# Rotating an 8192 x 8192 array by 90 degrees: 31 chunks of 1024 columns in place of 63 of 512, and a last macro tile that stays whole

## The chip, the cores and the metric

One core of one Trainium2 chip. The metric is device time in microseconds (us), median over runs. The program runs on this one core.

## The reference

```python
# x: 8192 x 8192 float32, k = 1
def reference(x, k):
    return np.rot90(x, k)      # out[i, j] = x[j, 8191 - i]
```

There is no arithmetic: 268.44 MB are read and 268.44 MB written, and on the way each 128 x 128 block is turned.

## The kernel before

The array is cut into 16 macro tiles of 1024 rows by 4096 columns. A macro tile has 8 **row tiles** (128 rows x 4096 columns, one load of 2 MiB each) and gives 8 **output groups** (512 columns of the input, one store of 2 MiB each), numbered 0 to 7.

- The SP queue loads row tiles into two load buffers (`a_pool`; some of the first eight loads go into output buffers that are still free).
- VectorE copies a loaded row tile, column order within blocks reversed, into **chunks** (`r_pool`). A load buffer is free again when all chunks of its row tile are copied.
- TensorE transposes blocks from chunks into PSUM. A chunk is free when all its columns have been transposed.
- ScalarE evicts PSUM into one of three output buffers (`o_pool`) and issues the store.

```python
W = 4096
CH = 512
a_pool = ctx.enter_context(tc.tile_pool(name="a_pool", bufs=2))
r_pool = ctx.enter_context(tc.tile_pool(name="r_pool", bufs=63))
o_pool = ctx.enter_context(tc.tile_pool(name="o_pool", bufs=3))
# ...
# load, for each row tile t of a macro tile:
nc.sync.dma_start(out=a[:], in_=x[r0 + t * P : r0 + (t + 1) * P, c0 : c0 + W])
for j in range(W // CH):
    ar = r_pool.tile([P, CH // P, P], dt, tag="ar")
    nc.vector.tensor_copy(out=ar[:], in_=a[:, j * CH : (j + 1) * CH]...[:, :, ::-1])
    chunks[t, j] = ar
# ...
# store, for each output group i (two halves h of two 128-column blocks):
if i == 0 and (rt == RT or r0 + rows < N):
    for t in range(rt):              # group 0: row tile by row tile, as they come in
        transposes(t, range(G))
# ... groups 1 to 7: block by block over all row tiles
nc.scalar.copy(o[:, G - PW - h : G - h, :], ps[h // PW])
nc.scalar.dma_start(out=dst, in_=o[:, G - done : G - done + S, :])
```

A macro tile of 8 row tiles needs 64 chunks of 512 columns and the pool has 63. And group 0 transposes row tile by row tile while they are loaded, so with chunks of 512 columns (one group wide) the chunks of group 0 are given back during the load, from the first row tile on. The last macro tile is split into two of 4 row tiles (`LAST = [4, 4]`), so that storing its first half overlaps loading its second.

## Time and profile before

| | before |
|---|---|
| median time | 1267.35 us (6 runs, 1266.35 to 1267.61) |
| transfers, 200 to 1200 us | 429 GB/s |
| VectorE copies | 1024 of 512 columns, 421 ns each, busy 355.4 us (28%) |
| ScalarE waiting for TensorE | 29.0 us, 10 times |
| ScalarE waiting for stores to land | 727.0 us, 118 times |

Transfers run at one flat rate and every engine waits for them. The lines are shown in the prediction. A row of the waits reads: who waited, for whom, total us, times, longest; a ScalarE wait for a store to land means that all three output buffers are filled or under way, which is the healthy state here: stores are always pending.

### The profile page before, as it was taken

The numbers are of one execution on the slowest core, as the hardware profiler recorded it, in microseconds if no ns is written. First come the engines' busy times: TensorE is split into PE (matmuls) and PEld (weight loads), VectorE is DVE, ScalarE is ACT, GpSimd is POOL, SyncE is SP. The second block draws the span as 40 slices with busy tenths as digits, with TensorE's granted clock in tenths as the row PEclk, the third lists the DMA queues.
The fourth block names the chain that finished last, engine by engine and source line by source line (L and its number), as shares of the span: only waits on it lengthen the run. The fifth ranks groups of instructions, "written<-read, shape, count | busy, mean of one in ns | idle before, by whom it ended". The sixth has DMA issues, their size and how long they took to land.

```text
span 1266.1 us, 10392 instructions
## 1 busy us (share of the span) xinstructions
PE 718.2 (57%) x4096; PEld 678.6 (54%) x4096; DVE 355.4 (28%) x1024; ACT 466.7 (37%) x257; POOL 0.7 (0%) x6
## 2 busy tenths in 40 slices
PE   1554565556656665556555665555655656556673
PEld 1543455555555555456554655555655655556562
DVE  4423223222232223222232223322232222322210
ACT  0432433433333333343334333343333433343363
POOL 0000000000000000000000000000000000000000
PEclk9977877777776777867778678677686686776797
DMA  9999999999999999999999999999999999999997
GB/s 399 426 428 430 428 429 427 430 429 429 429 429 429 430 428 427 430 429 430 428 430 428 429 429 428 430 428 428 430 430 428 429 429 428 428 428 428 427 399 328
DMA packets 37345, 537.55 MB, mean 425 GB/s; under 512 B 4144, under 2 KB 4144, under 8 KB 4144
## 3 DMA queue, kind: packets, MB, share of 16 engines
q10 hardware_dynamic: 18864, 268.44, 50.0%
q1 hardware_dynamic: 18432, 268.44, 49.7%
q8 instruction: 32, 0.52, 0.2%
q14 instruction: 17, 0.14, 0.0%
HBM read 268.44 MB, written 268.44 MB: 424 GB/s over the span
## 4 chain that ended last, share of the span: by engine, by line
DMA 82%; ACT 14%; PE 1%; issue 1%; ACTq 1%; DVE 0%; SPq 0%
DMA out_dram<-ot 79%; ACT ot L169 14%; DMA a<-in_x_dram 3%; PE pt L148 1%; ACTq L177 0%; DVE ar L108 0%; ACTq L169 0%; SPq L102 0%
## 5 line engine op out<-in xcount | busy, mean ns | idle before, releaser
L148 PE MATMUL pt<-ident,ar 128*128 128x128 f32 x4096 | 718.2, 356 | 528.0 <-ACT ot L169 487.6
L148 PEld LDWEIGHTS pt<-ident,ar 128*128 128x128 f32 x4096 | 678.6, 191 | 567.4 <-ACT ot L169 521.4
L169 ACT COPY ot<-pt 128x2048 f32<-128x2048 f32 x256 | 465.4, 1869 | 756.7 <-DMA out_dram<-ot 727.0
L108 DVE COPY ar<-a 128x512 f32<-128x512 f32 x1024 | 355.4, 421 | 861.1 <-DMA a<-in_x_dram 524.0
L169 ACT ACT_TABLE_LOAD x1 | 1.3, 1283 | 25.5 <-DVE ar L108 25.5
masks.py:199 POOL TENSOR_SCALAR_AFFINE_SELECT ident<-ident 128x128 f32<-128x128 f32 x1 | 0.3, 292 | 0.1
masks.py:197 POOL MEMSET ident<- 128x128 f32 x1 | 0.2, 204 | 0.3 <-POOLq L217 0.3
L217 POOL MEMSET const-bfloat16-1.0<- 128x1 bf16 x1 | 0.1, 102 | 0.0
L217 POOL MEMSET const-uint8-127<- 128x1 uint8 x1 | 0.1, 102 | 0.0
L217 POOL MEMSET const-float32-0.0<- 128x1 f32 x1 | 0.1, 99 | 0.2 <-issue 0.2
L217 POOL MEMSET const-float32-1.0<- 128x1 f32 x1 | 0.1, 99 | 0.0
## 6 DMA issues: line engine op xcount, KB each, us to landing
a<-in_x_dram SPq DMA_DIRECT2D x128, 2048.0 KB, 16.8
out_dram<-ot ACTq DMA_DIRECT2D x125, 2048.0 KB, 25.5
out_dram<-ot ACTq DMA_DIRECT2D x6, 1024.0 KB, 27.3
```

Of the source, the lines that this page charges most:

```text
L108: nc.vector.tensor_copy(out=ar[:], in_=a[:, j * CH : (j + 1) * CH].rearrange("r (b m) -> r b m", m=P)[:, :, ::-1],)
L148: nc.tensor.transpose(ps[w // PW][:, PW - 1 - w % PW, t * P : (t + 1) * P], chunks[t, g * P // CH][:, g % (CH // P), :], ident,)
L169: nc.scalar.copy(o[:, G - PW - h : G - h, :], ps[h // PW])
L217: nc = _bacc.Bacc("TRN2", target_bir_lowering=False, num_devices=1)
```

## The change

What it seems to be for: half as many VectorE copies and a simpler end. With 1024 columns a chunk serves two output groups, a macro tile needs 32 chunks, and the pool has 31.

```diff
-LAST = [4, 4]
-CH = 512
+CH = 1024
 ...
-    tiles = [(r0, RT, c0) for r0 in range(0, N, R) for c0 in range(0, M, W)]
-    r0, _, c0 = tiles.pop()
-    for n in LAST: ...
+    return [(r0, RT, c0) for r0 in range(0, N, R) for c0 in range(0, M, W)]
 ...
-    r_pool = ctx.enter_context(tc.tile_pool(name="r_pool", bufs=63))
+    r_pool = ctx.enter_context(tc.tile_pool(name="r_pool", bufs=31))
 ...
-            S = PW if lead or (end and r0 + rows == N and g0 + G == W // P) else G
+            S = PW if lead or (end and (i == 0 or g0 + G == W // P)) else G
 ...
+    for m in tiles:
+        store(*m, load(*m), m == tiles[-1])
```

(The generators that interleaved the two half tiles are gone; cuts are marked.)

More of the change, by code (lines that the diff above doesn't have):

```diff
@@ L47, in macro_tiles @@
 def macro_tiles(N, M):
-    tiles = [(r0, RT, c0) for r0 in range(0, N, R) for c0 in range(0, M, W)]
-    r0, _, c0 = tiles.pop()
-    for n in LAST:
-        tiles.append((r0, n, c0))
-        r0 += n * P
-    return tiles
+    return [(r0, RT, c0) for r0 in range(0, N, R) for c0 in range(0, M, W)]
 @with_exitstack
@@ L104, in load @@
             )
-            yield chunks
             for j in range(W // CH):
@@ L114, in load @@
                 chunks[t, j] = ar
-            yield chunks
+        return chunks
     def store(r0, rt, c0, chunks, end):
@@ L179, in store @@
                     )
-            yield
     tiles = macro_tiles(N, M)
-    *most, before_last, last = tiles
-    for m in most:
-        *_, chunks = load(*m)
-        for _ in store(*m, chunks, False):
-            pass
-    *_, chunks = load(*before_last)
-    outputs = store(*before_last, chunks, True)
-    rows = load(*last)
-    for _ in range(2 * last[1] - 1):
-        next(rows)
-    next(outputs)
-    chunks = next(rows)
-    for _ in outputs:
-        pass
-    for _ in store(*last, chunks, True):
-        pass
+    for m in tiles:
+        store(*m, load(*m), m == tiles[-1])
 _INS = ['x', 'k']
```

## The prediction

> **What bounds the kernel now.** I read the page first (busy shares and the row of GB/s), then the waits, then one stretch of the timeline in mid-run, then a table of windows over the start and the end. The page:
>
> ```profile
> span 1266.1 us, 10392 instructions
> PE 718.2 (57%) x4096; PEld 678.6 (54%) x4096; DVE 355.4 (28%) x1024; ACT 466.7 (37%) x257; POOL 0.7 (0%) x6
> ...
> GB/s 399 426 428 430 428 429 427 430 429 429 429 429 429 430 428 427 430 429 430 428 430 428 429 429 428 430 428 428 430 430 428 429 429 428 428 428 428 427 399 328
> DMA packets 37345, 537.55 MB, mean 425 GB/s; under 512 B 4144, under 2 KB 4144, under 8 KB 4144
> ```
>
> No engine is busy for more than 57%, and the transfers run flat at 427 to 430 GB/s in 36 of 40 slices. Only the first two slices (the second by a hair) and the last two are lower. So the kernel is a copy through the chip at the rate of the transfers, with an edge at each end. The waits (who waited for whom, total us, times, longest) say the same:
>
> ```profile
> ACT ot L169 <- DMA out_dram<-ot: 727.0, 118, 11.0
> DVE ar L108 <- DMA a<-in_x_dram: 524.0, 82, 10.2
> ...
> DVE ar L108 <- PE pt L148: 337.1, 49, 7.7
> ```
>
> ScalarE waits for stores to land (an output buffer), VectorE waits for loads, and 49 times for TensorE, which is the wait for a free chunk. One cycle of the timeline in mid-run (start, duration, then the instructions and the idle time before):
>
> ```profile
> 587.95 5.28 PE L148 MATMUL pt<-ident,ar 128*128 128x128 f32 x32 [3.02 <-ACT ot L169]
> 589.69 0.55 ACTq L177 DMA_DIRECT2D out_dram<-ot  x1
> 593.21 2.78 DVE L108 COPY ar<-a 128x512 f32<-128x512 f32 x8 [7.08 <-PE pt L148]
> 595.79 3.63 ACT L169 COPY ot<-pt 128x2048 f32<-128x2048 f32 x2 [6.13 <-DMA out_dram<-ot]
> ```
>
> Each 9.8 us one output group (32 transposes, two evictions, a 2 MiB store) leaves, its end frees the 8 chunks of its columns, and VectorE copies one row tile's worth (8 chunks) into them, which frees a load buffer. The next cycles start at 603 and 613 us: one store and one load per 9.8 us, 4.19 MB in 9.8 us = 428 GB/s. The windows (width; busy us of the engines; granted clock, share and GB/s last):
>
> ```profile
> 200.00:1100.00 900.00, 527.74 (x2914) 501.79 (x2912) 254.88 (x736) 332.63 (x184) 0.00 (x0) 0.74 1.01 429
> ...
> 1205.00:1210.00 5.00, 1.28 (x9) 0.89 (x9) 1.61 (x5) 3.63 (x2) 0.00 (x0) 0.90 0.94 398
> 1210.00:1215.00 5.00, 3.98 (x24) 3.75 (x24) 1.29 (x4) 1.42 (x1) 0.00 (x0) 0.76 0.94 400
> 1215.00:1220.00 5.00, 3.92 (x34) 3.64 (x35) 1.49 (x5) 4.33 (x4) 0.00 (x0) 1.00 0.80 338
> ...
> 1258.00:1260.00 2.00, 0.00 (x0) 0.00 (x0) 0.00 (x0) 0.00 (x0) 0.00 (x0) 0.50 0.39 160
> 1260.00:1262.00 2.00, 0.00 (x0) 0.00 (x0) 0.00 (x0) 0.00 (x0) 0.00 (x0) 0.50 0.15 61
> ```
>
> The budget, as time lost against 429 GB/s: 537.55 MB / 429 = 1253.0 us of pure transfer. Start, 0 to 6 us at 106, 287 and 393 GB/s: 2.3 lost. The three windows from 1205 to 1220, as the last load lands: (31 + 29 + 91) x 5 / 429 = 1.8. From 1220 to 1258, stores alone at 413 to 419: 1.1. From 1258 to the end, a few of the 16 transfer engines finishing (160, 61, 41 and 8 GB/s): 8.1 - 1.3 = 6.8. Sum 12.0, so 1265.0 of the 1266.1.
>
> **What the Trainium skill says.** "DMA: Bandwidth & Descriptors", section "Where 436 GB/s comes from", puts the ceiling of the 16 ports at 435.2 GB/s; the trace's 429 is 98.6% of it, so nothing in this change can make the middle faster by as much as 2%. The same page, "Queues, rings and completion order", says that each transfer engine takes turns, packet by packet, between the queues that have work; the trace agrees as far as loads and stores each move 2.1 MB per 9.8 us. It follows that an empty load queue hands its share to the stores and costs nothing while stores are pending. "VectorE: DVE Perf Modes", section "Mode 2×_2P", says that an fp32 copy within SBUF uses both ports for two elements a cycle; here 512 columns take 421 ns, less than the 533 ns of one element per cycle at its 0.96 GHz, so the copy is in that mode.
>
> **The change, part by part.**
> 1. *Half as many copies, twice as wide.* Eight narrow copies take 2.77 us, 346 ns each. Two per cycle, 512 columns are 267 ns, leaving 79 ns fixed (an estimate). A wide one then takes 613 ns, four take 2.45 us: 0.32 us less per row tile, 128 x 0.32 = 41 us of VectorE in all. VectorE is 28% busy and waits for loads, so nothing of it is on the path. On the path only once: TensorE's first work on the eighth row tile waits for the first chunk, 0.27 us later, so the first store goes 0.3 us later. Loads are under way then: 0 to 0.3.
> 2. *Coarser release.* A chunk of 1024 columns serves two output groups, so chunks come free 8 at a time after every second group (19.6 us), and 8 chunks are two row tiles. A macro tile needs 32 and has 31: its last chunk waits for its own second group. So of each 8 freed chunks one completes a half-copied row tile, four take the next, three begin a third. Two loads are issued together each 19.6 us in place of one per 9.8. The sum of bytes per 19.6 us is the same and three stores of 2.1 MB are kept in flight, so inside a macro tile nothing is lost. At its end: before, the load of the eighth row tile is issued after group 6 of 0 to 7; now after group 7, one group (9.8 us) later. By the medians in the page (16.8 us from issue to landing), counted from group 6's store issue: TensorE done +3.7, last chunk copied and load issued +4.4, landed +21.2, first chunk copied and transposed +23.4, evicted and stored +27.1; before, output buffers let that store go at +19.6. The stores thus fall 7.5 us behind, 1.6 MB at their 214 GB/s, out of about 5.4 MB in flight (25.5 us to landing). The queue shrinks but does not run dry. But transfer engines do not run level: in the final drain some are done 6 us before others, and in 1205 to 1220 the rate fell with stores still in flight. So a shallow queue loses a little; I put 0.1 us on each of 15 boundaries, 1.5 us, a choice between 0 and 0.7.
> 3. *The last macro tile whole.* Its last load has the same lag: after it is issued there remain about 6.6 MB of stores and up to 3 MB of loads, 22 us at 429, and the first half of its first output goes at about +17 us. That first half, new here, goes 1.9 us (one eviction) before the whole would. So a dip like today's 1.8 us, perhaps 0.5 more. From there groups come each 4.3 us (3.64 of eviction and 0.67 of idle, the rows from 1222 on), a store takes 4.9 us at 429: stores stay ahead of need.
> 4. *Longer runs in the tail's stores.* Half tiles write runs of 512 numbers (2 KiB), whole ones 1024 (4 KiB); issuing one of the former takes 1.0 to 1.1 us in the tail, of the latter 0.55. Stores alone lose 1.1 us today; I take 0.5 back.
> 5. *Drain*: also two half stores at the end; 6.8 stays.
>
> Sum: 1266.1 + 0.3 + 1.5 + 0.5 - 0.5 = 1267.9 of profiled span. The times lie 1.2 above the span (1267.27 against 1266.1), so **1269 us**.
>
> **The rivals.**
> - *The load queue starves at each boundary* (a wait for a chunk takes the place of the wait for a load). For it: 49 waits for TensorE already, and the release comes half as often. Against: bytes are conserved while stores are pending. If stores ran dry for 2 us at each of 15 boundaries: 30 us, 1299. I hold that for 6 in 100.
> - *A cleaner tail*: no dip at the last load, 4 KiB runs at the full rate, a shorter drain since queues are issued faster. Worth 1.8 + 1.1 + some 3: 1262. For: today's tail has twice the descriptors per byte. Against: the later last load.
> - *VectorE's saving shows*: 41 us less. Against: 861 us of its span is idle, and transfers are at 429. No gain.
> - *The whole tile's tail is exposed*: the stores drain before its first output is ready. At worst 5 us idle: 1274.
>
> **Range and chances.** Low 1262 from the cleaner tail, high 1280 from 0.7 us at each boundary plus 1 us in the tail. Faster by over 2% would need 1242, below the 1253 of pure transfer: 0.01. Slower by over 2% needs 1292.6, 25 us, or 1.6 us at each boundary: 0.06. The rest, 0.93, is within 2%.
>
> **What would show it.** VectorE 512 copies near 690 ns and about 314 us busy; TensorE and ScalarE counts unchanged; 124 stores of 2048 KB and 8 of 1024. Middle slices 427 to 430. VectorE's waits for TensorE longer singly (toward 19 us); bursts of copies in pairs of row tiles. Wrong if middle slices fall below 425 with ScalarE waiting for TensorE or VectorE (starved stores), or if the last three slices differ by over 4 us of transfer.

## The result, and the profile after

**1297.22 us** median (6 runs, 1294.35 to 1298.62) against 1267.35. The ratio is 1.0236, 95% interval 1.0223 to 1.0249: slower by 2.4%, outside the predicted range of 1262 to 1280.

The page after, first the span, then the GB/s in 40 slices, then VectorE's group (output, input, count; busy us, mean ns; idle before and its releaser):

```profile
span 1296.7 us, 9805 instructions
...
GB/s 400 425 429 428 428 429 418 429 387 417 428 395 429 413 422 428 388 430 409 413 429 389 429 414 422 430 393 429 411 416 428 411 428 401 427 429 407 430 333 379
...
L100 DVE COPY ar<-a 128x1024 f32<-128x1024 f32 x512 | 320.1, 688 | 935.2 <-DMA a<-in_x_dram 785.6
```

The flat row of 427 to 430 is gone. From the seventh slice on it dips, at 387 to 418, about every second or third slice, that is once in some 81 us, which is a macro tile. From 200 to 1200 us the mean is 416 GB/s, so (429 - 416) / 429 x 1000 = 30.3 us are lost in that stretch alone: nearly all of the 30.6 us between the spans. In section 4 of the page, the chain of work that ended last, stores took 79% of the span before; after, loads take 70% and stores 4%: the loads now set the time. The waits after:

```profile
DVE ar L100 <- DMA a<-in_x_dram: 785.6, 107, 12.7
ACT ot L161 <- DMA out_dram<-ot: 411.9, 64, 10.8
...
ACT ot L161 <- PE pt L140: 370.7, 64, 24.2
...
DVE ar L100 <- PE pt L140: 149.6, 22, 10.3
```

ScalarE now waits 370.7 us for TensorE (29.0 before), up to 24.2 us at a time: there was nothing to evict. VectorE's waits for TensorE, the ones for a free chunk, have become *fewer* and smaller in sum (149.6 against 337.1). A sum of waits does not say what a wait costs. One boundary between macro tiles, in the timeline (start, duration, instructions, then idle before them and its end):

```profile
662.71 0.55 ACTq L169 DMA_DIRECT2D out_dram<-ot  x1
...
663.90 2.50 DVE L100 COPY ar<-a 128x1024 f32<-128x1024 f32 x4 [7.22 <-DMA a<-in_x_dram]
673.64 2.50 DVE L100 COPY ar<-a 128x1024 f32<-128x1024 f32 x4 [7.24 <-DMA a<-in_x_dram]
...
683.41 1.90 DVE L100 COPY ar<-a 128x1024 f32<-128x1024 f32 x3 [7.27 <-DMA a<-in_x_dram]
...
684.89 3.63 ACT L161 COPY ot<-pt 128x2048 f32<-128x2048 f32 x2 [22.21 <-PE pt L140]
...
688.55 0.55 ACTq L169 DMA_DIRECT2D out_dram<-ot  x1
...
692.21 3.10 DVE L100 COPY ar<-a 128x1024 f32<-128x1024 f32 x5 [6.90 <-PE pt L140]
```

The last store of the old macro tile is issued at 662.71. At that point the new tile's sixth row tile has not been copied; the eighth comes at 683.41. ScalarE waits 22.21 us, and the next store goes at 688.55. The eighth row tile is copied in 3 + 1 chunks: the fourth must wait until TensorE is done with this tile's own group 1, at 692.21 (the x5 is that chunk and the next row tile). Until then the load buffer is held. The chain of work that ended last runs through exactly this wait (start, duration, what):

```profile
666.43 16.89 DMA a<-in_x_dram
...
686.81 5.38 PE pt L140 x25
692.21 0.70 DVE ar L100
692.93 11.67 DMA a<-in_x_dram
```

The load of the eighth row tile is issued at 666.43. The next load into the same buffer can only go at 692.93, after the last chunk's copy: 26.5 us later, in place of two cycles of 9.75, so 7 us late. In the DMA queues of 690 to 694 us (packets, MB, share of the 16 engines' time; q10 carries the stores, q1 the loads) practically no load data move:

```profile
q10 hardware_dynamic: 97, 1.59, 94.2%
q1 hardware_dynamic: 1, 0.00, 0.0%
```

And the windows over the same boundary and over the tail (last three figures: granted clock, DMA share, GB/s):

```profile
688.00:691.00 3.00, 3.00 (x16) 3.00 (x15) 0.00 (x0) 1.00 (x2) 0.00 (x0) 0.50 0.59 251
691.00:694.00 3.00, 3.00 (x26) 3.00 (x25) 1.79 (x3) 2.42 (x2) 0.00 (x0) 0.87 0.97 410
694.00:697.00 3.00, 2.65 (x23) 2.17 (x21) 1.31 (x3) 2.33 (x2) 0.00 (x0) 1.00 1.01 350
697.00:700.00 3.00, 2.56 (x23) 2.52 (x24) 0.00 (x0) 2.33 (x3) 0.00 (x0) 1.00 1.11 322
...
1244.00:1250.00 6.00, 2.18 (x9) 1.78 (x10) 1.90 (x3) 2.98 (x2) 0.00 (x0) 0.50 0.43 180
1250.00:1262.00 12.00, 11.19 (x78) 10.68 (x77) 0.69 (x1) 8.03 (x5) 0.00 (x0) 0.79 0.74 307
```

The windows from 685 to 703 us ran at 415, 251, 410, 350, 322 and 399 GB/s. The deficits against 429 are 14, 178, 19, 79, 107 and 30, so 427 x 3 / 429 = 3.0 us for this boundary. Less than half of it (14 + 178) falls before 691 us, where the queues had run out; the rest comes from 691 to 703 us, where the transfer engines count as busy (shares 0.97 to 1.11) and yet move less (last section). Thirteen boundaries between 200 and 1200 us show the same copy cut by a wait for TensorE; 30.3 / 13 = 2.3 us each. In the tail 1244 to 1262 us lost 3.5 + 3.4 = 6.9 us, against 1.8 at the same event before; the drain at the end is shorter (3.3 against 6.8 lost).

### The profile page after: what moved, and what is told of

It is laid out like the page before. It is cut to its first block, busy times and chain, and to the rows that moved or that the text cites. A ratio compares the mean times of both kernels' runs of the same rounds, so it can differ in the third digit from the quotient of the medians.

```text
span 1296.7 us, 9805 instructions
## 1 busy us (share of the span) xinstructions
PE 659.2 (51%) x4096; PEld 608.0 (47%) x4096; DVE 320.1 (25%) x512; ACT 467.9 (36%) x257; POOL 0.7 (0%) x6
## 4 chain that ended last, share of the span: by engine, by line
DMA 74%; PE 8%; DVE 8%; ACT 6%; issue 2%; ACTq 0%; DVEq 0%; SPq 0%
DMA a<-in_x_dram 70%; PE pt L140 8%; DVE ar L100 8%; ACT ot L161 6%; DMA out_dram<-ot 4%; ACTq L169 0%; DVEq L100 0%; SPq L95 0%; ACTq L161 0%
## 5 line engine op out<-in xcount | busy, mean ns | idle before, releaser
L140 PE MATMUL pt<-ident,ar 128*128 128x128 f32 x4096 | 659.2, 334 | 621.9 <-ACT ot L161 354.3
L140 PEld LDWEIGHTS pt<-ident,ar 128*128 128x128 f32 x4096 | 608.0, 176 | 672.9 <-ACT ot L161 390.7
L100 DVE COPY ar<-a 128x1024 f32<-128x1024 f32 x512 | 320.1, 688 | 935.2 <-DMA a<-in_x_dram 785.6
```

The source lines that it names most:

```text
L140: nc.tensor.transpose(ps[w // PW][:, PW - 1 - w % PW, t * P : (t + 1) * P], chunks[t, g * P // CH][:, g % (CH // P), :], ident,)
```

## The experiments

**Theory A**, formed from the timeline: the last wide chunk of a macro tile waits for its own tile's group 1. That holds one of two load buffers, the loads fall behind by some us at each boundary and cannot catch up while stores take half of the transfers, and so the stores then run out of data. **Rival B**, from the prediction's part 2: coarser release, two row tiles at a time, is what costs. **Rival C**: the whole last macro tile. **Rival D**: the wait costs through something else than the load buffer, such as VectorE standing still behind it.

| run | chunks | load / output buffers | last tile | median us | ratio to before (95%) |
|---|---|---|---|---|---|
| the change | 31 wide | 2 / 3 | whole | 1297.22 | 1.0236 (1.0223 to 1.0249) |
| e1 | 31 wide | 2 / 3 | split | 1289.26 | 1.0174 (1.0159 to 1.0189) |
| e2 | 63 narrow | 2 / 3 | whole | 1267.06 | 0.9995 (0.998 to 1.001) |
| e3 | 30 wide + 3 narrow | 2 / 3 | whole | 1268.39 | 1.0005 (0.999 to 1.002) |
| e4 | 55 narrow | 2 / 3 | whole | 1295.01 | 1.0217 (1.02 to 1.0234) |
| e5 | 56 narrow | 2 / 3 | whole | 1267.43 | 0.9999 (0.9985 to 1.0014) |
| e6 | 55 narrow | 3 / 3 | whole | 1267.59 | 1.0001 (0.9984 to 1.0017) |
| e7 | 55 narrow | 3 / 3 | split | 1267.62 | 1.0002 (0.999 to 1.0015) |
| e8 | 31 wide | 3 / 2 | whole | 1269.45 | 1.0013 (0.9997 to 1.0028) |

All outputs are right. Narrow is 512 columns, wide 1024. Each ratio is against runs of the kernel before in the same batch (its medians were 1267.35 to 1267.55 us).

### e1: wide chunks, the last tile split as before

```diff
 # the kernel before
-CH = 512
+CH = 1024
-r_pool ... bufs=63
+r_pool ... bufs=31
```

> 31 chunks of 1024 columns, but the last macro tile in two halves as in the kernel before. Theory A (the cost sits at the boundaries between macro tiles: the last wide chunk of a tile waits for its own tile's second output group and holds a load buffer for that time): the boundaries still lose some 2.2 us each at 13 boundaries, so 1290 to 1297 us. Rival C (the cost is the whole last tile): 1266 to 1270 us.

Measured 1289.26, a fraction of a us below theory A's interval and far from rival C. The GB/s row dips about as often as in the changed kernel:

```profile
GB/s 399 425 427 431 429 428 427 429 394 418 427 395 429 419 412 430 411 428 411 422 431 386 430 411 412 430 410 429 397 417 427 393 430 417 408 428 408 430 423 381
```

From 200 to 1200 us it averages 417 GB/s, 28.0 us lost. So the wide chunks make most of the loss without the whole tile. The split tail takes back 8.0 us of it (1297.22 - 1289.26), which I had not expected: half tiles of 16 chunks never run out, so the last boundary, the changed kernel's gap of 6.9 us from 1244 to 1262 us, is missing in e1 (429 and 419 GB/s from 1240 to 1260 us).

### e2: narrow chunks, the last tile whole

```diff
 # the changed kernel
-CH = 1024
+CH = 512
-r_pool ... bufs=31
+r_pool ... bufs=63
```

> 63 chunks of 512 columns, last macro tile whole as in the changed kernel. Theory A: no boundary loss, only the tail differs, by its windows about 1 to 2 us: 1264 to 1271 us. Rival C: 1290 us or more.

Measured 1267.06: the whole last tile costs nothing when the loads are on time. Rival C falls. The whole tile costs only together with wide chunks (8.0 us, by e1), since it is one more tile whose loads come late. From 200 to 1200 us e2 runs at 429 GB/s.

### e3: wide chunks, but no wait for the own tile

```diff
 # the changed kernel
-r_pool ... bufs=31
+r_pool ... bufs=30
+n_pool ... bufs=3          # 512 columns each
 for j in range(W // CH):
+    if t == RT - 1 and j in (0, W // CH - 1):
+        # ... two copies of 512 columns into n_pool tiles
+        continue
 # ... the transposes take the half that they need
```

> The changed kernel with 30 wide chunks and 3 narrow ones, the narrow ones only for the first and last 1024 columns of the eighth row tile, so that its last copy waits for nothing but the eighth row's own first transposes; all other chunks stay wide and still come free in pairs of row tiles. Theory A: the copy of the eighth row tile is no longer cut 3 + 1, its load buffer is free at once, and the loss at the boundaries goes: 1264 to 1273 us. Rival B (the release by pairs, which lets the eighth load be issued only after group 7, is what costs, as argued in the prediction's part 2): stays at 1290 to 1298 us.

The narrow half chunk of group 0 comes back as soon as that row tile's first transposes are done, so the last copy no longer needs group 1. The chunks' share of SBUF rises from 124 to 126 KiB a partition, what the kernel before has. Measured 1268.39. At the boundary VectorE's timeline reads:

```profile
665.03 0.76 DVE L105 COPY an<-a 128x512 f32<-128x512 f32 x2 [7.21 <-DMA a<-in_x_dram]
665.71 1.29 DVE L115 COPY ar<-a 128x1024 f32<-128x1024 f32 x2
666.91 0.75 DVE L105 COPY an<-a 128x512 f32<-128x512 f32 x2
674.96 2.50 DVE L115 COPY ar<-a 128x1024 f32<-128x1024 f32 x4 [7.29 <-DMA a<-in_x_dram]
```

The eighth row tile is copied in one go and the next follows 9.9 us later, the ordinary pace. From 200 to 1200 us the rate is 428 GB/s. Chunks are still given back in pairs of row tiles, so rival B falls as the cause. It is not without effect: ScalarE still waits for TensorE at each boundary, here and in the changed kernel (first e3, then the changed kernel's fourth macro tile):

```profile
666.24 3.64 ACT L179 COPY ot<-pt 128x2048 f32<-128x2048 f32 x2 [12.20 <-PE pt L158]
280.24 3.63 ACT L161 COPY ot<-pt 128x2048 f32<-128x2048 f32 x2 [24.23 <-PE pt L140]
```

In e3 the wait settles at 12 to 13 us and the rate stays at 430 GB/s through it (655 to 677 us): stores take 25.7 us from issue to landing there (median), so those under way outlast the wait. In the changed kernel it grows over the first boundaries, 8.10, 17.17, then 24.23 us, and stays near 20 to 24: the rate is 432 GB/s around the first (111 to 133 us), 411 around the second and 346 around the third. So the queue of stores covers a wait of some 13 us and not one of 20.

### e4 and e5: one narrow chunk

```diff
 # e2
-r_pool ... bufs=63
+r_pool ... bufs=55         # e4;  56 in e5
```

> The narrow whole-tile kernel of the second run with 55 chunks in place of 63: no wide chunk anywhere and no release by pairs, but now 9 of a tile's 64 chunks are missing, of which 8 come free early from its first group and the ninth only from its second group. The last narrow chunk of each tile thus waits as the last wide one did in the changed kernel. Theory A: slow like the changed kernel, 1288 to 1300 us. Rival B, or a rival that it is the width of the copies as such: within 5 us of the second run.

> The run with 55 narrow chunks, with one more (56): now 8 of a tile's 64 chunks are missing, and all 8 come free from the tile's first group, the last of them about 1 us after the eighth row's first copy. One chunk of 2 KiB per partition decides. Theory A: the cut in the last copy goes and the time falls to 1264 to 1273 us. Rival (the loss grows smoothly with fewer chunks, because a row tile's copies are released a group later): about 1290 us, a 63rd to 55th step of 1/8 only taken back.

Group 0 gives back 8 chunks early. With 56 chunks a tile lacks 8, with 55 it lacks 9, and the ninth comes from group 1. One chunk of 2 KiB a partition makes 27.6 us (1295.01 against 1267.43). By a count of chunks, that one chunk also moves the load of the eighth row tile from after group 6 to after group 7, so this pair alone does not tell the two apart; e3, where the load stays after group 7 and the own wait is gone, does. In e4 the boundary looks like that of the changed kernel, with 7 + 1 narrow copies in place of 3 + 1 wide ones:

```profile
600.09 2.44 DVE L100 COPY ar<-a 128x512 f32<-128x512 f32 x7 [7.03 <-DMA a<-in_x_dram]
608.84 2.77 DVE L100 COPY ar<-a 128x512 f32<-128x512 f32 x8 [6.32 <-PE pt L140]
```

So it is neither the width of the copies nor the number of chunks as such: 56 and 63 cost the same. It is a step.

### e6: the wait stays, a third load buffer

```diff
 # e4 (55 narrow chunks)
-a_pool ... bufs=2
+a_pool ... bufs=3
```

> The run with 55 narrow chunks, with a third load buffer in the 16 KiB that the 8 chunks fewer left free. The wait of the last chunk for its tile's second group stays. Theory A in its full form (the wait costs because it holds one of two load buffers, so that the loads fall behind and the stores then have nothing to send): 1263 to 1272 us although the wait is still there. Rival D (the wait costs because VectorE[...] stands still, or because the last data of the tile come late): 1285 us or more.

Measured 1267.59: the loss is gone with the wait still there. The waits:

```profile
DVE ar L100 <- PE pt L140: 815.8, 137, 10.6
ACT ot L161 <- DMA out_dram<-ot: 728.4, 117, 10.8
```

VectorE waits for free chunks for 815.8 us, over five times as long as in the changed kernel, and it costs nothing: ScalarE again waits almost only for stores (for TensorE 29.0 us, as before). VectorE standing still (rival D) is harmless here. A third buffer would help late loads of any cause, so e6 shows that the wait costs only through the load buffers; that it is the own-group wait which makes the loads late is e3's part.

### e7: can this beat the kernel before?

```diff
 # the kernel before
-r_pool ... bufs=63
+r_pool ... bufs=55
-a_pool ... bufs=2
+a_pool ... bufs=3
```

> The kernel before (narrow, split last tile) with 55 chunks and three load buffers: a try for something that beats both. Where loads run ahead, the dip of about 1.8 us as the last load lands may go; the rest is at the rate of the transfers. Theory A: 1263 to 1268 us. If a held load buffer is not what matters, the last-chunk wait (55 chunks) costs as in the earlier run and 1285 us or more comes out.

Measured 1267.62 over five rounds: the same as before. Nothing tried beats the kernel before by anything clear of the noise. Of its 1266.1 us of span 1253 are transfer at 429 GB/s, so there was 1% to be had at most.

### e8: the changed kernel, a load buffer for an output buffer

```diff
 # the changed kernel
-a_pool ... bufs=2
+a_pool ... bufs=3
-o_pool ... bufs=3
+o_pool ... bufs=2
```

> The changed kernel, 31 wide chunks and the last-chunk wait as they are, with one of the three output buffers turned into a third load buffer. Theory A: the loads no longer fall behind; if two output buffers still keep stores in flight, 1266 to 1275 us. If two are too few (ScalarE must evict for 3.6 us between a landing and the next store, while a store alone takes 4.9), the stores now run dry inside the tiles and it stays at 1285 us or above: then the third buffer's use for wide chunks is not shown by this run.

Measured 1269.45, with 31 wide chunks and the last-chunk wait untouched, and one 16 KiB buffer only moved. From 200 to 1200 us it runs at 428 GB/s. The waits (first two) are of the healthy kind again, and now the prediction's picture of 5 + 3 copies per pair of row tiles appears in its timeline:

```profile
ACT ot L161 <- DMA out_dram<-ot: 728.7, 116, 11.7
DVE ar L100 <- PE pt L140: 683.5, 61, 18.5
```

## Why the prediction was wrong, point by point

- **What bounds the kernel, and the budget of the edges**: right. The middle can only lose, and what was lost is lost transfer: 30.3 us between 200 and 1200 us.
- **Part 1, the copies**: right. 688 ns measured for about 690, busy 320.1 us for 314. The delay of 0.27 us is there (TensorE starts 0.75 us after the first copy of the eighth row tile, 0.48 before), but that row tile landed 0.56 us earlier, so the first store was issued at 47.60 us against 47.90. None of it mattered.
- **Part 2, the release: the step that failed.** The text says that the last chunk "waits for its own second group" and then gives that wait no price. It priced only the other consequence, the load issued after group 7 in place of group 6, and concluded that the queue of stores "shrinks but does not run dry". Counted from group 6's store issue (653.09 us in the boundary above) it put the next tile's load of the eighth row tile at +4.4 and its first store at +27.1. Measured: the load at 666.43, +13.3, and the store at 688.55, +35.5. That load was not late because of a chunk: the sixth row tile was copied at 663.90, when its own load landed. The loads were already some 9 us behind. My error was to treat each boundary as starting from the steady state of the kernel before. A held buffer of two delays the issue of the next load by about 7 us (the wait of 6.90 us). A part is made up at once, since that load then lands in 11.67 us and not in 16.89. The rest stays: while stores are pending the loads come at their half share, one per 9.8 us (663.90, 673.64, 683.41), which makes up nothing. So the delay is still there at the next boundary, and the waits of 8.10, 17.17 and 24.23 us (under e3) show it adding up until the stores run out. e3 shows that the own-group wait is the cause, e6 and e8 that it costs only by holding one of two load buffers, and e4 and e5 that neither wide chunks nor release by pairs are needed for it. e3 also shows that the priced part, the load after group 7, is worth next to nothing (1268.39): there the queue did shrink and not run dry, as the text said.
- **The price of 0.1 us per boundary** was in truth 2.3 us on average, 30.3 in sum from 200 to 1200 us.
- **Part 3, the whole tail**: a dip of about 2.3 us was foretold. With narrow chunks e2 lost 3.9 us from 1200 to 1230 (393 GB/s, then 333 from 1220 on), against 2.0 before, but a shorter drain made up for it. With wide chunks the same place lost 6.9 us, because the last tile's loads were late like all others.
- **Part 4, longer runs**: not shown. Stores alone ran at 422 GB/s from 1240 to 1256 us in e2 (4 KiB runs) and at 415 before (2 KiB runs), but e6, with 4 KiB runs too, ran at 416.
- **Part 5, the drain**: not the same; 3.3 us lost for 6.8. Why it is shorter was not tested.
- **The signs.** Wide copies, counts and store sizes came as written, and so did the sign of being wrong: middle slices at 387 to 418 GB/s with ScalarE waiting for TensorE. Longer waits for chunks (toward 19 us) and bursts in pairs of row tiles did not come: the longest was 10.3 us, since the loads were later than the chunks. Only e8, with a third load buffer, shows both.
- **The rivals.** The first, a load queue that starves at each boundary, is what happened in effect, and its 30 us and 1299 were near the 1297.22. That nearness is partly luck: it took 2 us at 15 boundaries, and it expected waits for chunks in place of waits for loads, where the runs show the reverse (waits for chunks fell from 337.1 to 149.6 us, those for loads rose from 524.0 to 785.6). It was given 6 in 100, because "bytes are conserved while stores are pending". True, but nothing guaranteed that they would be pending. The reading that might have warned: two load buffers, each 16.8 us in flight and 2.8 us in the copy, make 19.6 us, exactly two cycles of 9.8. Two buffers that are always in use must come to that sum, so it does not measure the slack (a load in flight may be waiting behind another); but it says that a buffer held for 7 us more must put back the load that comes next into it.

What stays open: how much of each delay the loads make up by themselves, and why transfers are slow for some us after a queue restarts (last section).

## What to carry to other kernels

When a pool is one or two buffers short of a whole tile, ask for its last allocation: which release does it wait for, and does that release depend on the tile being complete? If so, one chunk more or less can be a step of tens of us (e4 and e5), not a shade. Price a wait by the buffer that it holds and by how soon that buffer is needed for the next load: with 31 wide chunks, 683.5 us of waits for chunks cost nothing clear of the noise beside a third load buffer (e8), and 149.6 us without it cost 30.

## What the Trainium skill lacked or had wrong

- "DMA: Bandwidth & Descriptors", "Where 436 GB/s comes from": it says that for transfers between HBM and SBUF the HBM side, about 358 GB/s, binds. For this program on one core it did not: 429 GB/s, loads and stores together, for 1000 us. The page's ceiling of 435.2 and its own single-core figure of 425 (section "Measured") fit; a note beside that figure gives 358 only for both cores of a pair streaming, which the sentence itself does not say.
- The same page, "Queues, rings and completion order": packets from two queues in turns agrees with loads and stores of 2.1 MB each per 9.8 us. It does not say that traffic is slow where queues start anew. At the boundary above, 697 to 700 us, the share was 1.11 at 322 GB/s; in the trace's packet records a 16 KiB load packet took 1067 ns (median of those started from 698 to 700 us), 611 ns in steady running. The same holds 6 to 8 us after the cut copy at all 13 boundaries, with medians of 832 to 1072 ns. Nor are turns seen just before: from 695 to 699 us loads alone moved data (1.39 MB), though a store had been issued at 694.88; its first data packet came 4.8 us later, that of the store of 688.55 after 1.2 us. The cause was not tested.
- "VectorE: DVE Perf Modes", "Mode 2×_2P": two elements a cycle for an fp32 copy agrees, and holds for a reversed innermost order, which the section does not mention: 688 - 421 = 267 ns for 512 columns more, which is two columns per cycle of 0.96 GHz; the fixed part of a copy's own duration is then 421 - 267 = 154 ns, of which about half is hidden when copies follow each other (the prediction's 79).
- No page has a rule for a pool that is a few chunks short of a tile: 56 chunks 1267.43 us, 55 chunks 1295.01 us.
